# A hybrid encoder layer on one core: for 17 weight units of the down projection, the low half is made by an accumulating DMA

## The chip, the cores and the metric

The kernel runs on one core of one Trainium2 chip. The metric is the device time of one execution in microseconds (us), taken as the median of several runs. The engines are called PE (TensorE), DVE (VectorE), ACT (ScalarE), POOL (GpSimd) and SP (SyncE, which here only issues DMAs). The core has 16 DMA engines, which all its DMA queues share.

## The reference, cut to what matters

One layer over 256 tokens of width 2048: an input projection to eight groups of 1024 columns, two parallel head groups (a gated recurrence and a differential attention), an output projection with residual, then a SwiGLU feed-forward part with 5632 hidden columns:

```
mixed = jnp.concatenate([o_hg, o_da], axis=-1)
x = x + jnp.einsum('bsc,cd->bsd', mixed, w_out[l])
h = rmsnorm(x, norm_ffn_w[l])
u = jax.nn.silu(jnp.einsum('bsd,df->bsf', h, w_gate[l])) * jnp.einsum('bsd,df->bsf', h, w_up[l])
x = x + jnp.einsum('bsf,fd->bsd', u, w_down[l])
```

All of it is in float32. The change touches only the last line, the down projection.

## The kernel before, in words

**Products.** Every projection keeps its accuracy by splitting both operands into a high part, rounded to the format fp32r in which PE multiplies, and a low part, which is the rest. `product` (in the section printed below) makes three matmuls for each pair of a weight row block and a token block: high by high, high activation by low weight, low activation by high weight. These are lines 304, 305 and 306 of the profile. A matmul has 128 x 128 weights of PE (the activations) and 512 moving columns (the model's weights).

**Units.** The model's weights come in units of 128 partitions x 1024 numbers, 4 KB per partition and 512 KB in all. A unit holds two row blocks (KU = 2) of 512 columns (NC). There are 256 tokens in two blocks, so one unit feeds 2 x 2 x 3 = 12 matmuls. `Stream` hands out the units in the order of the whole program: input projection, output projection, gate and up weights in turns, and at the end 88 units of the down weights. These are four chunks (NCH_D) of 512 output columns with 22 units each; they are called chunk 0 to chunk 3 here.

**What a unit goes through.** `load` issues its DMA on SP's queue (L86) into one of five buffers named `raw`. `split` rounds it on ACT into `hi`, profile name whi (L98), and subtracts on DVE `lo` = `raw` - `hi`, profile name wlo (L99). The tiles whi and wlo have three buffers each. After the DVE subtraction the raw buffer is free for the unit five places on. `next`, called when `product` comes to unit u, first calls load up to u + 6 and then split up to u + 1.

**What sets the order.** The code runs in a framework that tracks which instruction needs which data, puts in the waits, and schedules each engine's queue from a list: what is ready first in its own timeline goes first, and the splits stand under a higher priority. So an engine's order need not be the order of the code. Each queue then runs strictly in its order on the chip. Side work (transposes, heads) is spread through the products by `pump`; in the down projection only chunk 0 has any. At the end of each chunk DVE adds the accumulators to the residual `xsb` (L650) and SP stores them (L651).

**Space.** The split activations of the feed-forward part, h2_hi and h2_lo, are two tiles of 128 x 16 x 256 numbers (tags "hhi" and "hlo"). They are last read by the last up product, just before the down projection.

Of the kernel before, what the change touches and what calls it, by code (L numbers as in the profile page):

```python
# [11 lines left out]
F32 = mybir.dt.float32  # L12
F32R = mybir.dt.float32r
BF16 = mybir.dt.bfloat16
U8 = mybir.dt.uint8
AF = mybir.ActivationFunctionType
ALU = mybir.AluOpType
# [3 lines left out]
P = 128  # L21
SEQ = 256
TT = SEQ // P
NC = 512
# [6 lines left out]
X_CUTS = [2, 2]  # L31
KU = 2
RAW_BUFS, HL_BUFS, HAT_BUFS = 5, 3, 5
EVERY_IN, EVERY_OUT, EVERY_FFN, WIDTH = 1, 1, 2, 2
LB_FLOOR = 1e-30
LB_CEIL = 1.0 - 1e-6
# [9 lines left out]
def encoder_layer(ctx: ExitStack, tc: tile.TileContext, xT, xr, w_in, w_out, w_gate, w_up, w_down,  # L46
                  nmix_w, params,
                  dist, masks, out):
    nc = tc.nc
    NK = xT.shape[1]  # L50
# [4 lines left out]
    NCH_D = w_out.shape[0]  # L55
    NF = w_gate.shape[0]
    NKF = NF * HPC
# [5 lines left out]
    big = ctx.enter_context(tc.tile_pool(name="big", bufs=1))  # L63
# [9 lines left out]
    class Stream:  # L73
        def __init__(self, srcs):
            self.srcs, self.raw, self.parts = srcs, {}, {}
            self.nl = self.ns = self.at = 0

        def cuts(self, u):

# [2 lines left out]
        def load(self, upto):  # L82
            while self.nl <= min(upto, len(self.srcs) - 1):
# [3 lines left out]
                self.raw[self.nl] = raw  # L87
                self.nl += 1

        def split(self, upto):  # L90
            self.load(upto)
            while self.ns <= min(upto, len(self.srcs) - 1):
                raw = self.raw.pop(self.ns)
                hi = wpool.tile([P, KU, NC], F32R, tag="whi", name="whi", bufs=HL_BUFS)
                lo = wpool.tile([P, KU, NC], F32R, tag="wlo", name="wlo", bufs=HL_BUFS)
                with tc.high_priority():
                    for k in self.cuts(self.ns):
                        nc.scalar.copy(out=hi[:, k, :], in_=raw[:, k, :])  # L98
                        self.last_split = nc.vector.tensor_tensor(out=lo[:, k, :], in0=raw[:, k, :],  # L99
                                                                  in1=hi[:, k, :].bitcast(F32), op=ALU.subtract)  # L100
                self.parts[self.ns] = (hi, lo)
                self.ns += 1
# [24 lines left out]
    srcs = []  # L127
# [15 lines left out]
    stream = Stream(srcs)  # L143
# [16 lines left out]
    for n in X_CUTS + [KG] * (NKG - 1):  # L160
# [4 lines left out]
        upto = min(-(-k0 // KU) - 1, RAW_BUFS - 1)  # L165
# [124 lines left out]
    def product(a_hi, a_lo, ks, accs, every):  # L290

        nu = len(ks) // KU
        slot = 0
        for i in range(nu):
            whi, wlo = stream.next()
            for tt in range(TT):
                acc = accs[tt]
                for k in range(KU):
                    kk = ks[i * KU + k]
                    hi = a_hi[:, kk, tt * P:(tt + 1) * P]  # L300
                    lo = a_lo[:, kk, tt * P:(tt + 1) * P]
                    first = i == 0 and k == 0
                    last = i == nu - 1 and k == KU - 1
                    nc.tensor.matmul(out=acc, lhsT=hi, rhs=whi[:, k, :], start=first, stop=False)  # L304
                    nc.tensor.matmul(out=acc, lhsT=hi, rhs=wlo[:, k, :], start=False, stop=False)  # L305
                    nc.tensor.matmul(out=acc, lhsT=lo, rhs=whi[:, k, :], start=False, stop=last)  # L306
                    slot += 1
                    if every and slot % every == 0:
                        pump()

    def new_accs(other=False):
        pool, tag = (ps_sc, "sc") if other else (ps_mm, "mm")
        return [pool.tile([P, NC], F32, tag=tag, name="acc") for _ in range(TT)]
# [307 lines left out]
    def put_u(f, u):  # L621

        ut = ffn.tile([P, HPC, SEQ], F32, tag="ut", name="ut")
        yield from squares(ut, u)
        for k2 in range(HPC // 2):
            us = ut[:, k2 * 2:k2 * 2 + 2, :]
            ksl = slice(f * HPC + k2 * 2, f * HPC + k2 * 2 + 2)
            nc.scalar.copy(out=u_hi[:, ksl, :], in_=us)
            nc.vector.tensor_tensor(out=u_lo[:, ksl, :], in0=us, in1=u_hi[:, ksl, :].bitcast(F32), op=ALU.subtract)
            yield  # L630

    for f in range(NF):
        accs = new_accs()
        product(h2_hi, h2_lo, list(range(NK)), accs, EVERY_FFN)
        u = ffn.tile([P, TT, NC], F32, tag="u", name="u")
# [6 lines left out]
                                           in1=u[:, tt, :], op0=ALU.mult, op1=ALU.mult)  # L642
        side.append(put_u(f, u))

    for c in range(NCH_D):
        accs = new_accs(other=c % 2 == 0)
        product(u_hi, u_lo, list(range(NKF)), accs, EVERY_FFN if c == 0 else 0)
        for tt in range(TT):
            xs = xsb[:, tt, c * NC:(c + 1) * NC]
            nc.vector.tensor_tensor(out=xs, in0=accs[tt], in1=xs, op=ALU.add)  # L650
            nc.sync.dma_start(out=out[tt * P:(tt + 1) * P, c * NC:(c + 1) * NC], in_=xs)  # L651
# [53 lines left out]
```

## Time and profile before

| what | value |
|---|---|
| median of 3 runs | 1246.73 us (1246.51 to 1247.34) |
| the profiled execution, its own time | 1247.31 us |
| its span, first to last instruction | 1245.5 us |
| around the span | 1.8 us |
| PE busy | 1233.1 us, 99% of the span |
| DVE, ACT, POOL busy | 862.0, 644.2, 36.6 us |
| granted TensorE clock | 1.000, the upper level (2.4 GHz), in the whole span |

The profile is one execution. Busy is the time in which an engine has an instruction running; for PE the recorded matmuls overlap (each lasts some 390 ns, and a new one begins every 227 ns), so the pace is read from start to start. "Idle before" in a row is the time the engine stood before these instructions, and the name behind the arrow is who ended it. Landing of a DMA is the time from its issue to the arrival of all its data.

### The profile page before, as it was taken

How to read it: one execution, taken by the hardware profiler on the slowest of the kernel's cores; microseconds unless marked ns; L12 is line 12 of the kernel's file. 1: busy time of each engine (PE TensorE's matmuls, PEld its weight loads, DVE VectorE, ACT ScalarE, POOL GpSimd, SP SyncE). 2: the span in 40 equal slices, each digit the busy share in tenths (PEclk: the TensorE clock that was granted, in tenths of full speed). 3: DMA queues.
4: the chain of work that ended last, by engine and by line, in shares of the span. 5: the costliest groups of instructions: out<-in, count | busy, mean ns of one | idle time of the engine just before them, and what ended most of it. 6: DMA issues, size and time to landing. Idle time of an engine off the chain costs nothing.

```text
span 1245.5 us, 15502 instructions
## 1 busy us (share of the span) xinstructions
PE 1233.1 (99%) x5661; PEld 1019.6 (82%) x5661; DVE 862.0 (69%) x1286; ACT 644.2 (52%) x933; POOL 36.6 (3%) x42
## 2 busy tenths in 40 slices
PE   8999999999999999999999999999999999999998
PEld 6778887878888888888888888888888888888887
DVE  6698989698998965757657766765776674444443
ACT  6656755766775665654344344434434443433332
POOL 0000111000012000000000000000000000000000
PEclk9999999999999999999999999999999999999999
DMA  8755345436444555555655556555655556656662
GB/s 300 261 193 169 136 136 186 169 136 202 153 136 152 169 169 169 174 194 190 197 190 192 197 189 200 189 198 189 195 192 192 196 192 197 205 199 206 192 213 86
DMA packets 64812, 230.48 MB, mean 185 GB/s; under 512 B 7264, under 2 KB 7392, under 8 KB 64736
## 3 DMA queue, kind: packets, MB, share of 16 engines
q1 hardware_dynamic: 64592, 229.49, 56.0%
q8 instruction: 44, 0.72, 0.2%
q14 instruction: 32, 0.26, 0.1%
q10 hardware_dynamic: 144, 0.01, 0.0%
HBM read 227.37 MB, written 2.10 MB: 184 GB/s over the span
## 4 chain that ended last, share of the span: by engine, by line
PE 88%; DVE 7%; DMA 1%; issue 1%; ACT 1%; POOL 0%; SPq 0%; ACTq 0%; DVEq 0%; POOLq 0%
PE acc L305 28%; PE acc L306 28%; PE acc L304 28%; DVE wlo L99 3%; DVE zt L327 3%; PE sc L401 2%; ACT whi L98 1%; DMA xt<-in_xT 1%; DMA vec<-in_params 1%; PE oa L510 1%; PE og L435 0%; PE tpx L605 0%; DMA raw<-in_w_in 0%; PE sca L476 0%; PE sca L478 0%
## 5 line engine op out<-in xcount | busy, mean ns | idle before, releaser
L99 DVE TENSOR_TENSOR wlo<-raw,whi 128x1024 fp32r<-128x1024 f32 (+1 forms) x425 | 518.7, 1221 | 342.7 <-ACT whi L98 341.0
L98 ACT CAST whi<-raw 128x1024 fp32r<-128x1024 f32 (+1 forms) x425 | 445.9, 1050 | 508.9 <-PE acc L306 486.5
L305 PE MATMUL acc<-wlo,h_hi 128*128 128x512 f32 x1216 | 476.3, 392 | 4.4 <-DVE wlo L99 4.2
L306 PE MATMUL acc<-whi,h_lo 128*128 128x512 f32 x1216 | 473.6, 391 | 0.0
L304 PE MATMUL acc<-whi,h_hi 128*128 128x512 f32 x1216 | 439.2, 393 | 1.5 <-ACT whi L98 1.5
L305 PEld LDWEIGHTS acc<-wlo,h_hi 128*128 128x128 f32 x1216 | 228.4, 188 | 55.7 <-DVE wlo L99 10.3
L304 PEld LDWEIGHTS acc<-whi,h_hi 128*128 128x128 f32 x1216 | 227.9, 188 | 48.1 <-ACT whi L98 2.7
L306 PEld LDWEIGHTS acc<-whi,h_lo 128*128 128x128 f32 x1216 | 228.4, 188 | 46.5
L305 PE MATMUL acc<-wlo,u_hi 128*128 128x512 f32 x352 | 136.9, 389 | 0.0
L306 PE MATMUL acc<-whi,u_lo 128*128 128x512 f32 x352 | 136.9, 389 | 0.0
L304 PE MATMUL acc<-whi,u_hi 128*128 128x512 f32 x352 | 122.9, 389 | 0.0
L327 DVE STREAM_TRANSPOSE ut<-u 32x256 f32<-32x256 f32 x176 | 76.7, 436 | 3.4
L305 PEld LDWEIGHTS acc<-wlo,u_hi 128*128 128x128 f32 x352 | 66.1, 188 | 13.8
L306 PEld LDWEIGHTS acc<-whi,u_lo 128*128 128x128 f32 x352 | 66.1, 188 | 13.7
L304 PEld LDWEIGHTS acc<-whi,u_hi 128*128 128x128 f32 x352 | 66.0, 188 | 13.7
L327 DVE STREAM_TRANSPOSE zt<-z 32x256 f32<-32x256 f32 x160 | 69.7, 436 | 2.8
L305 PE MATMUL acc<-wlo,m_hi 128*128 128x512 f32 x128 | 50.4, 394 | 0.0
L306 PE MATMUL acc<-whi,m_lo 128*128 128x512 f32 x128 | 50.0, 392 | 0.0
L304 PE MATMUL acc<-whi,m_hi 128*128 128x512 f32 x128 | 48.8, 396 | 0.0
L388 DVE TENSOR_TENSOR pk<-pk,t 128x256 f32<-128x256 f32 x112 | 44.0, 451 | 2.0 <-ACT hat L380 1.8
L380 ACT COPY hat<-pk 128x512 f32<-128x512 f32 x56 | 35.7, 666 | 11.8 <-PE sc L401 5.6
L401 PEld LDWEIGHTS sc<-hat 128*128 128x128 f32 x224 | 30.2, 191 | 2.6
(129 smaller groups left out, 641.0 us busy)
## 6 DMA issues: line engine op xcount, KB each, us to landing
raw<-in_w_in SPq DMA_DIRECT2D x127, 512.0 KB, 3.7
raw<-in_w_gate SPq DMA_DIRECT2D x88, 512.0 KB, 4.3
raw<-in_w_up SPq DMA_DIRECT2D x88, 512.0 KB, 4.4
raw<-in_w_down SPq DMA_DIRECT2D x88, 512.0 KB, 4.4
raw<-in_w_out SPq DMA_DIRECT2D x32, 512.0 KB, 3.7
xsb<-in_xr SPq DMA_DIRECT2D x4, 512.0 KB, 6.3
out<-xsb SPq DMA_DIRECT2D x8, 256.0 KB, 5.7
xt<-in_xT SPq DMA_DIRECT2D x3, 512.0 KB, 8.2
```

The lines of the kernel that those rows point to most:

```text
L98: nc.scalar.copy(out=hi[:, k, :], in_=raw[:, k, :])
L99: self.last_split = nc.vector.tensor_tensor(out=lo[:, k, :], in0=raw[:, k, :], in1=hi[:, k, :].bitcast(F32), op=ALU.subtract)
L304: nc.tensor.matmul(out=acc, lhsT=hi, rhs=whi[:, k, :], start=first, stop=False)
L305: nc.tensor.matmul(out=acc, lhsT=hi, rhs=wlo[:, k, :], start=False, stop=False)
L306: nc.tensor.matmul(out=acc, lhsT=lo, rhs=whi[:, k, :], start=False, stop=last)
L327: nc.vector.transpose(out=d, in_=s)
L380: nc.scalar.copy(out=sub_ap(hat, 0, [[SEQ, 2], [2 * m, nb], [m, 2], [1, m]]), in_=sub_ap(pk, 0, [[2 * SEQ, 2], [2 * m, nb], [SEQ + m, 2], ...
L388: nc.vector.tensor_tensor(out=ap, in0=ap, in1=tap, op=ALU.mult)
L401: nc.tensor.matmul(out=sc[:, j, :], lhsT=kk[:, js], rhs=qq[:, js], start=True, stop=True)
L510: nc.tensor.matmul(out=o[:, tt, :], lhsT=st[:, j, tt * P:(tt + 1) * P], rhs=v[:, j, cs], start=j == 0, stop=j == TT - 1)
```

## The change

Seventeen units of the down projection (in chunk 1 every fourth of the 22 units, six in all; in chunk 2 every second, eleven in all) are split in another way. ACT rounds raw into hi as before, then ACT writes the negative of hi into lo, and an accumulating DMA issued from POOL adds raw onto lo inside SBUF. Their hi and lo stand in four pairs of slots of their own, in the place of h2_hi and h2_lo. This is done up to three units (AHEAD) before the split of the ordinary units. Chunks 0 and 3 stay as they are.

```
+AHEAD = 3
...
+            self.slots, self.by_dma = [], set()
...
+        def split_by_dma(self, u):
+
+            raw = self.raw.pop(u)
+            hi, lo = self.slots[self.nd % len(self.slots)]
+            self.nd += 1
+            with tc.high_priority():
+                nc.scalar.copy(out=hi, in_=raw)
+                nc.scalar.activation(out=lo, in_=hi.bitcast(F32), func=AF.Copy, scale=-1.0)
+                nc.gpsimd.dma_start(out=lo, in_=raw, accum_op=ALU.add)
+            self.parts[u] = (hi, lo)
+
         def split(self, upto):
             self.load(upto)
+            for u in sorted(self.by_dma):
+                if u <= upto + AHEAD and u < self.nl and u in self.raw and self.slots:
+                    self.split_by_dma(u)
             while self.ns <= min(upto, len(self.srcs) - 1):
+                if self.ns in self.parts:
+                    self.ns += 1
+                    continue
                 raw = self.raw.pop(self.ns)
...
+    d_hi = big.tile([P, NK * SEQ // (KU * NC), KU, NC], F32R, tag="hhi", name="d_hi")
+    d_lo = big.tile([P, NK * SEQ // (KU * NC), KU, NC], F32R, tag="hlo", name="d_lo")
+    stream.slots = [(d_hi[:, i], d_lo[:, i]) for i in range(NK * SEQ // (KU * NC))]
+    per = NKF // KU
+    first = len(srcs) - NCH_D * per
+    stream.by_dma = {first + per + i for i in range(0, per, 4)} | {first + 2 * per + i for i in range(0, per, 2)}
     for c in range(NCH_D):
```

## Rows read from the trace of the kernel before

**Rows 1.** The page, busy time, share of the span and instructions of each engine.
```profile
PE   1233.1 (99%) x5661; PEld 1019.6 (82%) x5661; DVE 862.0 (69%) x1286; ACT 644.2 (52%) x933; POOL 36.6 (3%) x42
```

**Rows 2.** Busy time by stretch, chunks 1, 2, 3; columns in the first line.
```profile
core 0: us, PE busy (x) PEld busy (x) DVE busy (x) ACT busy (x) POOL busy (x), PEclk, DMA share, GB/s
1061.80:1121.60 59.80, 59.80 (x265) 49.51 (x264) 28.11 (x25) 23.17 (x23) 0.00 (x0) 1.00 0.63 203
1121.60:1181.40 59.80, 59.80 (x265) 49.55 (x264) 28.12 (x25) 23.18 (x22) 0.00 (x0) 1.00 0.63 202
1181.40:1241.20 59.80, 59.80 (x264) 49.18 (x263) 26.00 (x23) 21.10 (x20) 0.00 (x0) 1.00 0.48 150
```

**Rows 3.** Timeline in chunk 1: PE, start and length of a unit's first pair.
```profile
1102.33 0.61 PE L304 MATMUL acc<-whi,u_hi 128*128 128x512 f32 x2
...
1105.05 0.61 PE L304 MATMUL acc<-whi,u_hi 128*128 128x512 f32 x2
...
1113.21 0.61 PE L304 MATMUL acc<-whi,u_hi 128*128 128x512 f32 x2
```

**Rows 4.** Groups of instructions by line, chunk 2 (1121.6 to 1181.4 us).
```profile
L99 DVE TENSOR_TENSOR wlo<-raw,whi 128x1024 fp32r<-128x1024 f32 x22 | 27.0, 1225 | 31.7 <-ACT whi L98 31.7
L98 ACT CAST whi<-raw 128x1024 fp32r<-128x1024 f32 x22 | 23.2, 1055 | 36.6 <-PE acc L306 36.6
```

**Rows 5.** Timeline of all engines in chunk 1: splits and loads.
```profile
1111.78 1.22 DVE L99 TENSOR_TENSOR wlo<-raw,whi 128x1024 fp32r<-128x1024 f32 x1 [1.49 <-ACT whi L98]
...
1113.03 3.05 SPq L86 DMA_DIRECT2D raw<-in_w_down  x2
...
1113.41 1.05 ACT L98 CAST whi<-raw 128x1024 fp32r<-128x1024 f32 x1 [1.67 <-PE acc L306]
...
1114.50 1.23 DVE L99 TENSOR_TENSOR wlo<-raw,whi 128x1024 fp32r<-128x1024 f32 x1 [1.50 <-ACT whi L98]
```

**Rows 6.** DMA queues and issues, chunk 2 (window 1121 to 1181 us).
```profile
q1 hardware_dynamic: 3483, 12.13, 62.8%
...
raw<-in_w_down SPq DMA_DIRECT2D x22, 512.0 KB, 4.5
out<-xsb SPq DMA_DIRECT2D x2, 256.0 KB, 5.4
```

**Rows 7.** Line 86 from 1040 to 1220 us: landing of its 66 loads.
```profile
DMA to landing us min/median/max: 3.1/4.4/6.4
```

**Rows 8.** DMA, the first 100 us in 40 slices of 2.5 us.
```profile
DMA  2999999997568999999860546165438288666656
GB/s 45 272 299 360 398 418 415 387 403 265 174 190 288 280 387 376 249 287 370 364 208 11 200 177 213 46 210 174 152 123 301 88 297 320 185 205 229 206 151 224
...
xt<-in_xT SPq DMA_DIRECT2D x3, 512.0 KB, 8.2
```

**Rows 9.** Timeline of all engines up to the start of chunk 0.
```profile
999.17 1.05 ACT L98 CAST whi<-raw 128x1024 fp32r<-128x1024 f32 x1 [1.67 <-PE acc L306]
...
1000.26 1.23 DVE L99 TENSOR_TENSOR wlo<-raw,whi 128x1024 fp32r<-128x1024 f32 x1 [1.49 <-ACT whi L98]
...
1001.40 0.74 DVE L641 SCALAR_TENSOR_TENSOR u<-acc,rstd,u 128x512 f32<-128x512 f32 x1
...
1001.69 0.39 PE L304 MATMUL acc<-whi,u_hi 128*128 128x512 f32 x1
```

**Rows 10.** Timeline of ACT in chunk 0: a slice of u_hi is written.
```profile
1021.89 1.14 ACT L628 CAST u_hi<-ut 128x512 fp32r<-128x512 f32 x2
```

More of the change, by code (lines that the diff above doesn't have):

```diff
@@ L75, in __init__ @@
             self.srcs, self.raw, self.parts = srcs, {}, {}
-            self.nl = self.ns = self.at = 0
+            self.nl = self.ns = self.at = self.nd = 0
+            self.slots, self.by_dma = [], set()
         def cuts(self, u):
```

## The prediction

> **What bounds the kernel now.** I first read the page's busy times [rows 1]: PE is busy for 99% of the span, DVE for 69%, ACT for 52%. A share over the whole span says little about the last stage, so I then cut the down projection into its chunks [rows 2]. In chunks 1 and 2, which the change touches, PE is busy for 59.80 of 59.80 us, at the full granted clock; DVE is busy for 28.1 us, ACT for 23.2, POOL for nothing, and the DMA engines for 63%. The timeline gives the pace [rows 3]: units begin at 1102.33, 1105.05 and, three later, 1113.21, so one unit takes 2.72 us, 22 units make 59.84 us, and that is the chunk's whole length. PE waits for nothing here. What the change takes off DVE is therefore off a path that ends early, and the question is only what it puts on.
>
> How early the path ends [rows 5]: two units before a unit is needed, a whi buffer comes free and ACT rounds (1113.41, 0.2 us after the unit of 1113.21 began); DVE ends at 1115.73. SP issues the load of the unit five places on right behind that, as the 1113.03 behind the 1113.00 shows. So ordinary low parts are there 2.9 us before PE wants them (2 x 2.72 - 2.5), and the load of unit w is issued 0.2 us before the start of w - 6 and lands, with 4.5 us [rows 6], 1.6 us after the start of w - 5. It is rounded only 0.2 us after the start of w - 2, so raw data lie ready for 6.8 us.
>
> **The change, part by part.** *Removed:* 17 subtractions of 1.225 us on DVE [rows 4], 20.8 us. DVE stood idle for 31.7 us of chunk 2 waiting for ACT, and PE never waited for it. Worth nothing to the end.
>
> *Added on ACT:* 17 more passes over 128 x 1024. The row for such a pass is the rounding, 1.055 us [rows 4], so 17.9 us, against 36.6 us in which ACT waited for PE in chunk 2 alone. Hidden in sum. In time: a DMA unit holds ACT for 2.1 us; an ordinary rounding that becomes ready at 0.2 us behind it would end 2.1 us later than now, inside the 2.9 us. Nothing, as long as ACT does not stand waiting for a load with an ordinary rounding queued behind it (a rival, below). The slots are slices of one tile; that the framework tracks slices is seen in chunk 0, where a slice of u_hi is written without a wait while PE reads others [rows 10]. So a slot waits for PE only where its own last unit, eight units back in chunk 2, is unread; that is long past.
>
> *Added on POOL's queue:* 17 DMA issues. POOL has nothing else to do there [rows 2], so nobody stands behind them. No row shows how long it takes to issue one: it goes into the latency below.
>
> *Added on the DMA engines:* 17 transfers of 512 KB that read raw, read lo and write lo. The trace has no accumulating transfer. Bounds come from the loads. One pass over 512 KB costs, by the share in chunk 2 (62.8% of 60 us for 12.13 MB [rows 6]), 37.7 x 0.524 / 12.13 = 1.63 us of all 16 engines; in the fullest stretch, five slices from 10 to 22.5 us at a mean of 404 GB/s [rows 8], 524288 / 404000 = 1.30 us. Low end: one pass, if the second read runs beside the first, 1.3 us. I take two passes, because the add must fetch two operands that are each as large as a load: 2.6 to 3.3 us. High end: four passes, 6.5 us, if the add itself goes slower than the bytes; nothing in the rows excludes it.
>
> A rule of the Trainium skill speaks to this price and against the change: "Collectives: The Full Stack", section "The bandwidth ceiling: the fold count and why AG ≠ RS ≠ AR", says that a reduction in the DMA engine needs two source reads, both on the same ring, and so delivers half the rate of a copy. By it the price would be the two passes, and no run here shows it yet.
>
> Now the budget. In chunk 1 four units (10.88 us) carry four loads and one add: 5 x 1.63 + 1.63 = 9.8 us. It fits. In chunk 2 two units (5.44 us) carry two loads and one add: 4 x 1.63 = 6.5 us, which is 1.08 us too much, eleven times, 11.9 us; or at the full stretch's rate 4 x 1.30 = 5.2 us, which just fits at 96%.
>
> The latency: a DMA unit's raw lands 1.6 us after the start of w - 5, two ACT passes and hand-overs take 2.2, so the add is issued at 3.8, and 5 x 2.72 - 3.8 = 9.8 us are left until PE starts w. A second limit holds in chunk 2, since raw stays taken until the add has landed. The load of w + 5 waits for that, the load of w + 6, again a DMA unit's, stands behind it on SP's queue, then come landing (4.5), ACT (2.2) and its own add. For six units in 16.3 us the add may take 16.3 - 0.35 - 4.5 - 2.2 = 9.2 us. What will it take? At least 3.1 us, as the fastest load [rows 7]. Loads take 4.5, and a second pass makes it 6.1: no wait. Where the queues were full, loads took 8.2 [rows 8]; with a second pass of 1.3 that is 9.5, just too long.
>
> **The sum.** Chunk 2 with two passes is the part that pays. At the full stretch's rate it fits, and only the latency limit is missed by 0.3 us per six units, some 1 us in all. At the share of the stage it lacks 11.9 us, of which the first 3.7 (9.8 - 6.1, the lead of a DMA unit) are used up unseen: 8.2 us. The loads of this stage are paced, so their share is likely to shrink somewhat when the queue is full, but the add is a new kind of traffic: I take 5 us, between the ends. Chunk 3 only catches up. The profiled execution, 1245.5 us of span and 1.8 around it, would become 1247.3 + 5.0 = 1252.3; it stands 0.6 above the median of the three runs, so the forecast is 1251.7 us.
>
> **The rivals.** *The add is hidden (no change).* If both reads and the write overlap, an add costs near one pass, chunk 2 needs 3 x 1.63 = 4.9 of 5.44 us, the add lands in about 5 us, and PE goes on at 2.72 us per unit: 1246.7. For it speaks that PE has no idle at all and each stage of the pipe has over 3 us of lead. The point from which it decides is the 5.44 us per pair and the 9.2 us of landing. The Trainium skill, "DMA: Bandwidth & Descriptors", section "Anatomy of one DMA — SWDGE (gpsimd) path", gives a POOL-issued transfer 2.0 us plus its bytes at 436 GB/s; by it a plain 512 KB copy would take 3.2 us, an estimate, and the latency would be no limit; no row has such a transfer.
>
> *The add is much slower than two passes.* At three, a pair takes 2 x 1.63 + 4.9 = 8.2 us, 2.7 over, eleven times 30; chunk 1 lacks 0.5 five times; less 3.7 of lead it is some 29 us: 1276. At four, 4.3 x 11 + 2.2 x 5 - 3.7 = 55: 1302. For it: no row has an add in a transfer. Against it: nothing but that the data volume asks for two.
>
> *ACT waits for loads.* In the code the DMA unit's rounding (up to u + 4) stands ahead of the ordinary one (u + 1). Were ACT's queue kept in that order, ordinary rounding, subtraction, load five on, and the two ACT passes would form a ring per pair in chunk 2: 1.06 + 1.23 + 4.5 + 2.1 = 8.9 us against 5.44, eleven times 3.45, less 3.7: +34, 1281. Against it: the scheduler takes what is ready. Where chunk 0 begins (1001.69), the subtraction for a unit two ahead ran at 1000.26, before L641 at 1001.40, though the code has L641 first [rows 9]; and an ordinary rounding is ready 0.2 us after a unit's start, a DMA unit's load lands 1.6 after one.
>
> *Faster.* PE has no idle in the stage, so only something outside it could give time; I see nothing. *That the change is not carried out* I exclude: at next(u) loads are known up to u + 6 and the ordinary splits stand at u + 1, so each of the 17 units is in raw when the test for u + 4 comes.
>
> **How the numbers follow.** A measurement of this kernel tells some 0.2%, 2.5 us, from no change. Forecast case (two passes, +1 to +8): 0.38, of which 0.05 lies within 2.5 us. Hidden: 0.34. Slow add: 0.16, half of it at three passes or less. ACT order: 0.09. Faster: 0.03. So slower 0.58, same 0.39, faster 0.03. The forecast case alone spans 1247.7 to 1255. The range starts at 1246.0, takes in the hidden case, and reaches to three passes, 1276; left out are the four-pass half (0.08), ACT order (0.09) and faster (0.03), 0.2 together.
>
> **What would show it.** Right: in chunk 2 the DMA share is at 0.9 or more, adds land in 8 to 11 us, PE shows idle time released by the adds there and none in chunk 1 or 3, and loads land later than 4.5 us. The hidden case: chunk 2 still lasts 59.8 us. Slow add: chunk 1 is longer too. ACT order: ACT's idle in chunk 2 is ended by raw loads, with adds landing early. The forecast is wrong if chunk 2 keeps its length, or if the wait is on anything but the adds.

## The result, and the profile after the change

The changed kernel took 1266.49 us (median of 4 runs, 1265.57 to 1267.48) beside 1246.81 for the kernel before (4 runs, 1246.51 to 1247.34): a ratio of 1.0158, with an interval of 1.0140 to 1.0175. That is 19.7 us slower, where the prediction had 5. The profiled execution took 1267.48 us with a span of 1265.7, 20.2 more than before in both.

First the page of the changed kernel: busy times, the group of the new roundings and the row of the adds among its DMA issues (KB each, median us to landing).

```profile
PE 1241.1 (98%) x5661; PEld 1022.2 (81%) x5661; DVE 840.8 (66%) x1269; ACT 658.0 (52%) x950; POOL 51.6 (4%) x59
...
L98 ACT CAST d_hi<-raw 128x1024 fp32r<-128x1024 f32 x17 | 17.8, 1049 | 76.8 <-DMA raw<-in_w_down 76.8
...
d_lo<-raw POOLq DMA_DIRECT2D x17, 512.0 KB, 7.1
```

Against [rows 1], DVE lost the predicted 21 us of work, and ACT was given 14. The line to stop at is the second: before 15 of the 17 new roundings ACT stood still until a load of raw weights had landed, for 76.8 us in all. In chunk 2 of the kernel before, roundings had waited for PE alone [rows 4].

Next chunks 0 to 3, by the windows view of the changed kernel, each from its first matmul to that of the next (a chunk has 264; the x counts also one that reaches into the stretch). Two short stretches inside chunk 2 follow.

```profile
core 0: us, PE busy (x) PEld busy (x) DVE busy (x) ACT busy (x) POOL busy (x), PEclk, DMA share, GB/s
1001.75:1061.87 60.12, 60.12 (x266) 49.47 (x264) 34.94 (x41) 24.98 (x25) 1.06 (x1) 1.00 0.62 189
1061.87:1134.50 72.63, 64.15 (x265) 50.16 (x264) 20.35 (x18) 29.37 (x30) 6.11 (x7) 0.98 0.73 210
1134.50:1201.66 67.16, 62.78 (x265) 51.38 (x264) 16.59 (x15) 30.29 (x30) 7.84 (x9) 0.95 0.97 273
1201.66:1261.50 59.84, 59.84 (x265) 49.36 (x263) 25.89 (x22) 21.10 (x20) 0.00 (x0) 1.00 0.44 146
...
1150.00:1165.00 15.00, 14.85 (x54) 12.02 (x55) 2.75 (x3) 6.13 (x7) 2.11 (x3) 0.81 0.98 276
...
1180.00:1190.00 10.00, 10.00 (x46) 8.28 (x45) 2.30 (x2) 6.04 (x7) 1.74 (x2) 1.00 1.03 297
```

Chunks 0 and 3 keep their length, but for 0.3 us. Chunk 1 takes 72.6 us and chunk 2 takes 67.2, where each took 59.8 [rows 2]: 12.8 and 7.3 us more, so the 20 us are all there, and most of them in chunk 1. Two things in these rows speak against the forecast. Chunk 1, which was to fit, has a PE idle for 8.5 us (72.63 - 64.15) while the DMA engines are busy for only 0.73 of the time. And from 1180 to 1190 us, at a DMA share of 1.03, PE has no idle at all.

PE's idle in the two chunks is 8.5 + 4.4 = 12.9 us. Of the other 7, some 4.3 go to matmuls at the lower clock. The rest are late starts that are not counted as idle, since a matmul is recorded as busy for some 390 ns and the next can begin after 227. The timeline of PE in the changed kernel (start, length, and in brackets the idle before and its releaser) shows the longest case:

```profile
1145.38 0.39 PE L323 MATMUL acc<-d_hi,u_hi 128*128 128x512 f32 x1
1150.15 0.79 PE L324 MATMUL acc<-d_lo,u_hi 128*128 128x512 f32 x1 [4.38 <-DMA d_lo<-raw]
1150.74 0.63 PE L325 MATMUL acc<-d_hi,u_lo 128*128 128x512 f32 x1
1151.17 0.63 PE L323 MATMUL acc<-d_hi,u_hi 128*128 128x512 f32 x1
```

Matmuls that began every 0.227 us begin every 0.43 behind the 4.38 us of idle, and the 15 us around them have a granted clock of 0.81: part of the stretch ran at 1.2 rather than 2.4 GHz. Thirteen matmuls ran so here and eight in chunk 1 (from 1118.2 to 1121.6 us the granted clock was 0.51). At 0.2 us more for each of the 21, that makes the 4.3 us.

Who is waited for? The waits of the changed kernel from 1055 to 1266 us (us in total, times, longest):

```profile
ACT d_hi L98 <- DMA raw<-in_w_down: 74.1, 14, 9.3
...
PEld acc L324 <- DMA d_lo<-raw: 8.2, 4, 4.8
...
PE acc L324 <- DMA d_lo<-raw: 6.5, 3, 4.4
PEld acc L323 <- ACT whi L117: 5.1, 3, 2.3
PEld acc L324 <- DVE wlo L118: 4.0, 5, 1.1
```

PE waits for adds three or four times, but as often for ordinary units, which no add touches: for ACT's whi and for DVE's wlo. Those are late because ACT was. The timeline of ACT in chunk 1 of the changed kernel shows how:

```profile
1076.28 1.05 ACT L98 CAST d_hi<-raw 128x1024 fp32r<-128x1024 f32 x1 [7.71 <-DMA raw<-in_w_down]
1077.23 1.04 ACT L117 CAST whi<-raw 128x1024 fp32r<-128x1024 f32 x1
1078.18 1.06 ACT L99 ACTIVATE d_lo<-d_hi 128x1024 fp32r<-128x1024 f32 x1
1079.14 1.98 ACT L117 CAST whi<-raw 128x1024 fp32r<-128x1024 f32 x2
1087.53 1.05 ACT L98 CAST d_hi<-raw 128x1024 fp32r<-128x1024 f32 x1 [6.41 <-DMA raw<-in_w_down]
1088.61 1.06 ACT L99 ACTIVATE d_lo<-d_hi 128x1024 fp32r<-128x1024 f32 x1
1089.58 1.98 ACT L117 CAST whi<-raw 128x1024 fp32r<-128x1024 f32 x2
1099.57 1.05 ACT L98 CAST d_hi<-raw 128x1024 fp32r<-128x1024 f32 x1 [8.02 <-DMA raw<-in_w_down]
...
1113.69 1.04 ACT L98 CAST d_hi<-raw 128x1024 fp32r<-128x1024 f32 x1 [9.28 <-DMA raw<-in_w_down]
```

This is the picture to remember. ACT stands for 6 to 9 us in front of a DMA unit's rounding whose data have not landed. The moment it gets through, the ordinary roundings queued behind run one after the other with no idle between: they had been ready, and stood behind an instruction that was not. Four units pass from one L98 to the next, and four units are 10.88 us of PE's work; from 1076.28 to 1113.69 the mean is 12.5.

The chain of waits of the changed kernel, in order of time (start, length, what), tells why the loads come late:

```profile
1088.61 1.07 ACT d_lo L99
...
1089.97 4.83 DMA d_lo<-raw
...
1094.81 4.74 DMA raw<-in_w_down
...
1099.57 0.04 ACT d_hi L98
...
1101.47 1.06 ACT d_lo L99
...
1102.82 7.08 DMA d_lo<-raw
...
1109.91 3.75 DMA raw<-in_w_down
...
1113.69 0.04 ACT d_hi L98
```

Negative, add, next load, next rounding: the load at 1094.81 starts when the add of 1089.97 lands, since it gets the raw buffer that this add was reading. The waits of SP's queue between 1045 and 1201 us say the same of all 17:

```profile
SPq L88 <- DMA d_lo<-raw: 67.4, 17, 8.2
```

Chunk 2 loses its time in one place, the 4.38 us of idle above. The chain there, by the same view:

```profile
1124.53 8.67 DMA d_lo<-raw
...
1133.22 5.85 DMA raw<-in_w_down
...
1142.35 7.76 DMA d_lo<-raw
...
1150.15 0.79 PE acc L324
```

The add of unit 44 (unit 0 is the first of the down projection) lands at 1133.20. Only then can the load of unit 48 start, which gets its buffer, and the add of unit 48 lands too late for PE. Unit 48 lasts from 1145.38 to 1155.01, 9.6 us in the place of 2.72: that is 6.9 of the 7.3 us of chunk 2.

From this came the theories for the experiments. **Theory A**: a ring through ACT's queue. A DMA unit's rounding waits there for its load, the ordinary roundings wait behind it, and the next DMA unit's load needs a buffer that those free. **Theory R**: what costs is the raw buffer that the add holds until it has landed. **Theory B**, that of the prediction: the DMA engines have more to move than fits.

### The profile page after: what moved, and what is told of

The parts are those of the page before. It is cut to its first block, busy times and chain, and to the rows that moved or that the text cites. A ratio compares the mean times of both kernels' runs of the same rounds, so it can differ in the third digit from the quotient of the medians.

```text
span 1265.7 us, 15537 instructions
## 1 busy us (share of the span) xinstructions
PE 1241.1 (98%) x5661; PEld 1022.2 (81%) x5661; DVE 840.8 (66%) x1269; ACT 658.0 (52%) x950; POOL 51.6 (4%) x59
## 4 chain that ended last, share of the span: by engine, by line
PE 79%; DMA 8%; DVE 8%; issue 2%; ACT 2%; SPq 0%; POOL 0%; ACTq 0%; POOLq 0%; DVEq 0%
PE acc L324 25%; PE acc L325 25%; PE acc L323 25%; DVE wlo L118 4%; DMA raw<-in_w_down 3%; DVE zt L346 3%; DMA d_lo<-raw 3%; PE sc L420 2%; ACT whi L117 1%; DMA xt<-in_xT 1%; DMA vec<-in_params 1%; PE oa L529 1%; DMA xsb<-in_xr 0%; ACT d_lo L99 0%; PE og L454 0%
## 5 line engine op out<-in xcount | busy, mean ns | idle before, releaser
L118 DVE TENSOR_TENSOR wlo<-raw,whi 128x1024 fp32r<-128x1024 f32 (+1 forms) x408 | 497.5, 1221 | 381.4 <-ACT whi L117 379.8
L117 ACT CAST whi<-raw 128x1024 fp32r<-128x1024 f32 (+1 forms) x408 | 427.3, 1049 | 438.0 <-PE acc L325 415.2
L324 PE MATMUL acc<-wlo,u_hi 128*128 128x512 f32 x284 | 111.9, 394 | 2.5 <-DVE wlo L118 2.5
L325 PE MATMUL acc<-whi,u_lo 128*128 128x512 f32 x284 | 111.1, 391 | 0.0
L323 PE MATMUL acc<-whi,u_hi 128*128 128x512 f32 x284 | 105.4, 394 | 3.8 <-ACT whi L117 3.8
L323 PEld LDWEIGHTS acc<-whi,u_hi 128*128 128x128 f32 x284 | 53.7, 189 | 16.4 <-ACT whi L117 5.1
L324 PEld LDWEIGHTS acc<-wlo,u_hi 128*128 128x128 f32 x284 | 53.9, 190 | 15.1 <-DVE wlo L118 4.0
L325 PEld LDWEIGHTS acc<-whi,u_lo 128*128 128x128 f32 x284 | 53.9, 190 | 11.3
L98 ACT CAST d_hi<-raw 128x1024 fp32r<-128x1024 f32 x17 | 17.8, 1049 | 76.8 <-DMA raw<-in_w_down 76.8
```

The source lines that it names most:

```text
L98: nc.scalar.copy(out=hi, in_=raw)
```

## The experiments

All ratios are to the kernel before, run beside each; the interval is 95%. Where an edit touches the down projection's splits, the scheduler writes ACT's queue anew, so what each kernel's queue is has to be read, not assumed. In the built programs it runs like this around units 30 and 34 of the down projection (D a DMA unit's rounding, neg its negative, N an ordinary rounding):

```
as changed                N27 D30 N28 neg N29 N31 D34 neg N32 N33
order                     N27 D30 neg N28 N29 N31 D34 neg N32 N33
add by DVE                N25 D30 neg N27 N28 N29 D34 neg N31 N32
narrow add                N25 D30 N27 neg N28 N29 D34 neg N31 N32
own raw, in order         N25 D30 neg N27 N28 N29 D34 neg N31 N32
later rounding            N27 N28 D30 neg N29 N31 N32 D34 neg N33
own raw, later rounding   N27 N28 D30 neg N29 N31 N32 D34 neg N33
own raw, 33 adds          N27 D30 neg N29 D32 neg N31 D34 neg N33
```

**The order in ACT's queue.** The DMA unit's rounding is issued behind the ordinary roundings that stand in the code at the same place.

```
             with tc.high_priority():
-                nc.scalar.copy(out=hi, in_=raw)
+                with tc.issue_after(self.last_cast.ins):
+                    nc.scalar.copy(out=hi, in_=raw)
...
-            for u in sorted(self.by_dma):
-                ...
             while self.ns <= min(upto, len(self.srcs) - 1):
...
+                        self.last_cast = nc.scalar.copy(out=hi[:, k, :], in_=raw[:, k, :])
...
+            for u in sorted(self.by_dma):
+                ...
```

> The ordinary rounding of the same step is put ahead of the DMA unit's on ACT's queue; the loads that wait for an add then are those of the next DMA unit itself (four in a row in chunk 1). Theory R (a ring through the raw buffer that an add holds: add 7.1 us, load 4.5, two ACT passes 2.2, POOL's hand-over 0.3, 14.1 us per four units against 10.88): chunk 1 stays long or gets longer, total 1264 to 1275 us. Theory A (ACT's queue: ordinary roundings stuck behind a rounding that waits for its load): chunk 1 falls back towards 60 us, total under 1258. Theory B (DMA bandwidth alone): as the changed kernel, 1266.

Measured: 1258.39 us, 1.0094 (1.0079 to 1.0109), which is 11.2 slower than before instead of 19.7. That is 0.4 us over what theory A allowed, and less than R and B had. With the same DMAs and the same work, the order is worth 8.5 us, so B, to which the order makes no difference, can't be the whole. But less moved in chunk 1 than was meant. At units 22, 38 and 42 the rounding did come behind an ordinary one. At 26 and 30 only the negative moved: it follows its rounding directly, so the add is issued one ordinary rounding (1.04 us) sooner. At 34 nothing moved. An add that is issued sooner also ends its hold sooner, so this run does not part A from R. Chunk 1 still takes 67.05 us here and chunk 2 66.62, and ACT still waits 66.2 us for loads.

**The add made by DVE.** The same work on ACT, but no transfer.

```
-                nc.gpsimd.dma_start(out=lo, in_=raw, accum_op=ALU.add)
+                nc.vector.tensor_tensor(out=lo, in0=raw, in1=lo.bitcast(F32), op=ALU.add)
```

> Same ACT work and order, but the add is done by DVE (about 1.2 us) in place of the DMA; the raw buffer is free again after it, and the DMA engines carry the loads alone. Theory R and theory B: 1247 to 1250 us, chunks 1 and 2 at 60 us each. Theory A: still long, 1258 to 1270, with ACT idle until raw loads land while ordinary roundings stand behind.

Measured: 1253.0 us, 1.0049 (1.0033 to 1.0066): 5.8 slower than before with not one accumulating DMA. All three had missed: R and B had it too low, A too high. The loss is all in chunk 1, which takes 67.28 us; chunk 2 takes 59.84. The queue is not quite that of the changed kernel: the rounding stands one place earlier (D30 ahead of N27). The chain of waits of this kernel in chunk 1 shows the ring bare:

```profile
1078.78 6.51 DMA raw<-in_w_down
...
1085.32 1.06 ACT d_hi L98
...
1086.39 1.07 ACT d_lo L99
...
1089.77 1.23 DVE wlo L118
...
1091.01 6.66 DMA raw<-in_w_down
...
1097.69 1.06 ACT d_hi L98
```

From one d_hi to the next, 12.37 us: two passes on ACT (2.1), the way through DVE's queue to the end of an ordinary subtraction (3.5, with its waits), and a load of 6.66. In the kernel before, a load took 4.4 [rows 7]. It is longer here, probably because the three ordinary units, let go together, free their buffers together: SP issued four loads within 3.7 us from 1088.74. With 4.4 in the place of 6.66 the ring would be 10.1 us and fit into 10.88. No run took the bunching away by itself.

**Own raw buffers for the DMA units.** The add then holds nothing that another load needs.

```
+                if self.nl in self.by_dma:
+                    raw = self.dpool.tile([P, KU, NC], F32, tag=("u", "ut")[self.nr % 2], name="raw")
+                    self.nr += 1
...
+    stream.dpool = ffn
```

> The DMA units load into four raw buffers of their own (in tiles of the feed-forward part that are free by then), so an add holds no buffer of the ring of five, and their loads come far ahead, so that ACT does not wait for them. Adds and bytes as in the changed kernel. Theories R and A: chunk 1 back at 60 us. Theory B for chunk 2 (6.2 to 6.5 us of DMA work per pair against 5.44): chunk 2 still 5 to 10 us long, total 1252 to 1257; without B 1247 to 1249.

Measured: 1255.18 us, 1.0065 (1.0050 to 1.0080). The loss moved. Chunks 1 and 2 both take 59.84 us, the full pace, with all 17 adds, where B had chunk 2 long. Chunk 0 takes 67.60: its PE is busy for only 54.57 of the 59.80 us to 1061.5, at a DMA share of 0.89. The loads into the free buffers were all issued early, in a bunch. The roundings of chunk 1's DMA units came early in ACT's queue with them, and ACT stood in front of four of these for 16.3 us. So the order changed along with the buffers, and the experiment was made again below with the loads in order.

**A narrow add.** Only the first 64 of 512 columns of each row block are added, 64 KB instead of 512.

```
+                nc.gpsimd.dma_start(out=lo[:, :, :64], in_=raw[:, :, :64], accum_op=ALU.add)
```

> The DMA adds only the first 64 of the 512 columns of each row block (the rest of the low part is left at minus the high part), an eighth of the bytes; ACT's work and order and the raw buffers as in the changed kernel. Theory B: 1247. Theory R: the add lands in some 4 us instead of 7.1, the ring of chunk 1 shrinks from 12 to under 10 us, total 1247 to 1254. Theory A: near 1260 or more.

Measured: 1261.3 us, 1.0117 (1.0100 to 1.0134). With an eighth of the bytes, 14.1 of 19.7 us remain, so B falls as the whole. These adds still took 4.8 us to land (median, 7.1 for the full ones). By chunks, chunk 2 is whole again (59.84 us) and chunk 1 is not better at all (72.54 beside 72.63). The queue is not that of the changed kernel either: in chunk 1 the roundings of units 30 and 34 stand one place earlier, so what the shorter hold gave there can't be told.

**A later rounding.** AHEAD is 2, with the order of the first experiment: a DMA unit's rounding comes behind that of the ordinary unit two places before it (N28 ahead of D30).

```
-AHEAD = 3
+AHEAD = 2
```

> AHEAD 2, and the DMA unit's rounding is tied behind the ordinary rounding of the unit two before it on ACT's queue; raw buffers, adds and bytes as in the changed kernel. Theory A (the loss is a ring: rounding of a DMA unit waits for its load, ordinary roundings queue behind it, and the load of the next DMA unit waits for a buffer that those free): one ordinary rounding fewer in the ring and the load less early needed, so the ring falls below 10.88 us per four units; total 1247 to 1253 us. Theory R (raw buffers held by the adds) and theory B (bandwidth): still 1258 or more, chunk 2 over 64 us.

Measured: 1252.22 us beside 1246.53, 1.0051 (1.0036 to 1.0066). ACT's waits for loads fall to 42.0 us. What is left stands before the adds: PE's two queues wait for them for 8.6 and 6.1 us. The total is as A had it, but by chunks only half of it: chunk 1 is nearly whole at 61.15 us, and chunk 2 still takes 66.28, as R and B had said (over 64). In chunk 2, where every second unit is a DMA unit, the edit moves little in the queue, and nothing from D52 on.

**Own raw buffers, loads in order.** As the third experiment, and each of these loads is issued behind the one before it.

```
+                    with tc.issue_after(self.last_load.ins) if self.nl in self.by_dma else ExitStack():
+                        self.last_load = nc.sync.dma_start(out=raw[:, k, :], in_=self.srcs[self.nl][:, k, :])
```

> As the run with raw buffers of their own, but the DMA units' loads keep their place in the order of loads instead of coming early in a bunch. The ring of five then serves ordinary units alone. Theories A and R: no ring is left, chunks 1 and 2 at 60 us each, total 1247 to 1249 us, with all 17 adds done. Theory B: chunk 2 longer, 1252 or more.

Measured: 1254.0 us, 1.0060 (1.0045 to 1.0075), a miss by 5 us of the time expected for it. Taking the hold away leaves 7.5 of the 19.7 us. Chunk 2, with the same adds and bytes, is whole at 59.84 us; the loss is in chunk 1, at 67.21. There ACT's roundings for DMA units start at 1069.04, 1080.88, 1092.47 and 1104.37, still 11.6 to 11.9 us apart, each behind 6.2 to 6.9 us of waiting for the load. So the ring of the DVE experiment is there without any hold. The queue is the likely reason of the miss (the tenth experiment bears it out): free of the hold, the DMA unit's rounding was put one place earlier than in the changed kernel, with three ordinary roundings behind it.

**Own raw buffers, 33 adds.** The same with every second unit of chunks 1, 2 and 3, so that only one ordinary rounding stands behind each DMA unit's, and nearly twice as many adds run.

```
+    stream.by_dma = {first + j * per + i for j in (1, 2, 3) for i in range(0, per, 2)}
```

> The same with every second unit of chunks 1, 2 and 3 as DMA units, 33 adds. It asks whether two loads and one add per 5.44 us fit the DMA engines over 180 us. Two passes at the stage's 1.63 us (6.5 us per pair): 33 x 1.08 - 10 = 25 us over before, 1272. At the full stretch's 1.30 (5.2 us per pair): it fits, 1247 to 1250.

Measured: 1246.93 us (10 runs) beside 1246.53 (13 runs), 1.0002 (0.9992 to 1.0012): nothing lost. Its first and its last 20 us of seven such stretches by the windows view (columns as above):

```profile
1061.50:1081.50 20.00, 20.00 (x90) 16.54 (x89) 6.01 (x6) 10.10 (x10) 2.61 (x3) 1.00 1.04 307
...
1181.40:1201.40 20.00, 20.00 (x90) 16.57 (x89) 5.59 (x5) 11.24 (x11) 3.48 (x4) 1.00 1.05 311
```

The DMA share is at 1.04 to 1.05 for 140 us on end, adds land in 8.5 us (median, up to 12.2), loads in 10.9, and PE has no idle. Two loads and an add per pair of units fit.

**A copy in the place of the add.** As the sixth experiment, with the low part overwritten by raw itself, to price the add.

```
-                nc.gpsimd.dma_start(out=lo, in_=raw, accum_op=ALU.add)
+                nc.gpsimd.dma_start(out=lo, in_=raw)
```

> As e6, but the POOL DMA copies raw over the low part instead of adding (the low part is then raw itself; the add alone is left out). The share of the DMA engines per transfer: if an add costs two passes and a copy one, 2.8 us per add against 1.4 to 1.6 per copy, and the landing shorter by 1 to 2 us. Time as e6.

Measured: 1251.23 us, one run. Its POOL queue from 1055 to 1200 us (packets, MB, share of 16 engines; then the issues, with the median landing):

```profile
q0 software_dynamic: 2304, 8.39, 15.7%
...
d_lo<-raw POOLq DMA_DIRECT2D x16, 512.0 KB, 5.5
```

and the same rows of the sixth experiment:

```profile
q0 software_dynamic: 2304, 8.39, 29.8%
...
d_lo<-raw POOLq DMA_DIRECT2D x16, 512.0 KB, 8.5
```

For the same 16 transfers a copy costs 0.157 x 145 / 16 = 1.42 us of the 16 engines, an add 0.298 x 145 / 16 = 2.70: a factor of 1.9.

**The two passes on POOL.** Nothing of the DMA units is left in ACT's queue.

```
+                nc.gpsimd.tensor_copy(out=hi, in_=raw)
+                nc.gpsimd.tensor_scalar(out=lo, in0=hi.bitcast(F32), scalar1=-1.0, scalar2=None, op0=ALU.mult)
```

> The DMA unit's two passes (rounding, negative) run on POOL in place of ACT, so ACT's queue holds ordinary roundings alone and nothing stands behind a DMA unit that waits for its load; five shared raw buffers and all 17 adds as in the changed kernel. Theory A (ACT's queue closes the ring): total 1247 to 1252 us, PE without idle in chunk 1. Theory R (the raw buffers held by adds are enough): 1257 or more.

Measured: 1272.55 us, 1.0203 (1.0183 to 1.0222). By the total, theory A missed by over 20 us and R's bound is met, but POOL is slow at this work. The groups of POOL (busy, mean ns) from 1050 to 1210 us:

```profile
L99 POOL TENSOR_SCALAR d_lo<-d_hi 128x1024 fp32r<-128x1024 f32 x17 | 52.4, 3110 | 0.6
L98 POOL CAST d_hi<-raw 128x1024 fp32r<-128x1024 f32 x16 | 19.0, 1185 | 53.4 <-DMA raw<-in_w_down 51.4 <-PE acc L325 2.0
```

A negative takes 3.1 us where ACT took 1.06, and in chunk 2, which takes 84.92 us, the adds come too late. But chunk 1 is nearly cured, though its adds hold shared buffers too: it takes 61.17 us (72.63 after the change). Taking the passes out of ACT's queue did that, together with the other order in which the shared buffers are then handed out.

**Own raw buffers and the later rounding together.**

> Raw buffers of their own with loads in order (as e6) and the DMA unit's rounding one ordinary rounding later on ACT's queue (as e5). Theory A: both halves of the ring of chunk 1 are shortened, 1246 to 1249 us. If instead a late add is what costs: the adds are issued up to 2.7 us later, PE would wait for d_lo in chunk 1 and the total stays at 1251 or more.

Its edit is that of the fifth and the sixth. Measured: 1247.87 us (10 runs) beside 1247.27 (14 runs), 1.0006 (0.9996 to 1.0015): all 17 adds are there and no loss that can be told. The timeline of ACT in its chunk 1:

```profile
1070.48 1.05 ACT L120 CAST whi<-raw 128x1024 fp32r<-128x1024 f32 x1 [1.67 <-PE acc L331]
1071.43 1.05 ACT L104 CAST d_hi<-raw 128x1024 fp32r<-128x1024 f32 x1
...
1081.36 1.05 ACT L120 CAST whi<-raw 128x1024 fp32r<-128x1024 f32 x1 [1.67 <-PE acc L331]
1082.31 1.05 ACT L104 CAST d_hi<-raw 128x1024 fp32r<-128x1024 f32 x1
```

Set it beside the ACT rows of the changed kernel. The d_hi rounding now starts without idle, right behind an ordinary one, every 10.88 us; the idle is released by PE again, as in [rows 4].

**Chunk 1 alone, chunk 2 alone.** by_dma keeps one of its two sets.

```
+    stream.by_dma = {first + per + i for i in range(0, per, 4)}
```

> Only the six units of chunk 1 (every fourth) go by DMA. Theory A: the ring of 12 us per four units against 10.88 costs most of what the changed kernel loses in chunk 1, some 6 to 10 us: 1253 to 1257 us.

```
+    stream.by_dma = {first + 2 * per + i for i in range(0, per, 2)}
```

> Only the eleven units of chunk 2 (every second) go by DMA, from a pipe that has its full lead. If the two chunks' losses add up, 1247 + 19.7 less what chunk 1 alone costs, so 1256 to 1260 us; if chunk 2 lost mainly because chunk 1 had used up the lead, 1247 to 1252 us.

Measured: 1255.98 us, 1.0076 (1.0057 to 1.0096), for chunk 1 alone; 1254.67 us, 1.0057 (1.0039 to 1.0075), for chunk 2 alone. The first is as expected, the second lies between its two cases. That is 8.7 and 7.4 over the 1247.27 beside them, 16.1 together, against 19.7. The six units of chunk 1 cost about as much as the eleven of chunk 2, the contrary of what a budget of bytes would give. The other 3.6 do not look like a lead that chunk 2 lacked: chunk 1 takes 67.78 us with its own six units alone and 72.63 in the changed kernel, where the first units of chunk 2 already stand in ACT's queue before chunk 1 ends (D44 ahead of N41). That this is the reason was not shown.

**What stands.** Four kernels make a table of the two causes, in us over the kernel before of the same job:

| | order left to the scheduler | DMA unit's rounding tied behind the ordinary one two units before |
|---|---|---|
| raw buffers shared | 19.7 | 5.7 |
| own raw buffers, loads in order | 7.5 | 0.6 |

The left column is not one order (its lower kernel has the rounding a place earlier), the right one is, in chunk 1. Either cure alone removes more than half, and only both remove it.

The two chunks tell why it takes both. These are their lengths in us in the profiled executions, one of each kernel (up to 3.2 us from the kernel's median time):

| | chunk 1 | chunk 2 |
|---|---|---|
| before | 59.84 | 59.84 |
| as changed | 72.63 | 67.16 |
| order | 67.05 | 66.62 |
| later rounding | 61.15 | 66.28 |
| the two passes on POOL | 61.17 | 84.92 |
| narrow add | 72.54 | 59.84 |
| add by DVE | 67.28 | 59.84 |
| own raw, in order | 67.21 | 59.84 |
| own raw, later rounding | 60.31 | 59.84 |

Chunk 2 is whole wherever no add holds a shared buffer, or holds it shorter, and nowhere else. There the cause is theory R, the raw buffer that is held until the add has landed. Chunk 1 comes near its length only where ACT's queue is another. There theory A is a cause: a ring of latencies of load, rounding and negative in ACT's queue, the ordinary roundings held up behind, and the next load. The two kernels with own buffers show it, since up to the end of chunk 1 their loads and buffers are the same and only ACT's order differs: 67.21 against 60.31.

How much the hold adds in chunk 1 of the changed kernel is open. The framework hands the shared buffers out anew in each kernel. In the changed one the loads of units 26, 38 and 42 get the buffer of the DMA unit before them (the chain of 1088.61 to 1113.69 above goes through such holds), and in the kernel of the later rounding no load of chunk 1's DMA units does, so that its 61.15 us are not the order's work alone.

No version beat the kernel before. The best two equal it, as they must with a PE that had no idle.

## Why the prediction was right and wrong

*What was taken away is worth nothing.* Right. DVE's 21 us are gone and no chunk is shorter for it.

*ACT's 17 passes are hidden.* In sum, yes: ACT stays at 52% of the span, and with all 17 passes the tenth experiment loses nothing. In place, no. This step carried the failure in chunk 1, which lost 12.8 of the 20 us: "Nothing, as long as ACT does not stand waiting for a load with an ordinary rounding queued behind it". That is what it did there. The rival for it had a chance of 0.09, because "the scheduler takes what is ready" and a DMA unit's load was reckoned to land later than an ordinary rounding becomes ready. The scheduler does so in its own timeline, and the queue that it wrote has the DMA unit's rounding first. Why its timeline has it so is open. What was shown is that tying it behind the ordinary rounding of the unit two before it, with own buffers, cures the loss.

The rival was also priced wrongly. Its ring went once per pair of chunk 2 (8.9 us for 5.44) and had no part in chunk 1. In truth one ring spans four units in chunk 1 and lasts 11.6 to 12.4 us even without the held buffer, with loads of 6.5 to 6.7 us in it (the chain of the DVE experiment), issued four together. The rival's time of 1281 was too high, and its place, chunk 2 alone, was wrong.

*The second limit of chunk 2*, that raw stays taken until the add has landed, was seen and rated at 1 us. This is the other step that failed: it is what chunk 2 lost, 7.3 us, and chunk 2 is whole in every kernel without it. The prediction had the load of the unit five on wait for the add, and so counted six units, 16.3 us, for one round. In the changed kernel the load of unit 48 waited for the add of unit 44. The round had four units, 10.88 us, and took 17.8 (from one add's issue to the other's, 1124.53 to 1142.35). At the later rounding the hold is worth 5.1 us in all (5.7 against 0.6).

*Two passes per add.* Right: 2.70 us in the sixth experiment and, from 33.1% of 145 us for 17 transfers, 2.82 in the changed kernel, inside the 2.6 to 3.3. A copy took 1.42. The Trainium skill ("Collectives: The Full Stack", section "The bandwidth ceiling: the fold count and why AG ≠ RS ≠ AR") states for the reduction of a collective that its add needs two source reads and so delivers half the rate of a copy; the factor of 1.9, of a plain accumulating DMA, agrees with it.

*The budget of chunk 2 lacks 1.08 us per pair.* This is the term from which the 5 us came, and it was wrong in whole. Under a full queue a load of the seventh experiment costs 0.548 x 145 us for 30.40 MB, 1.37 us per 512 KB, near the low end of 1.30 and not the 1.63 of a paced queue; its add costs 2.65. Two loads and an add are 5.39 of 5.44 us. "At the full stretch's rate it fits" was the right end, and the middle between the two was no safe choice: the share of a paced queue was no price here.

*The add's latency.* 7.1 us median, 4.8 to 9.1, below the first limit of 9.8 and the forecast of 8 to 11. The estimate from "DMA: Bandwidth & Descriptors" of the Trainium skill, section "Anatomy of one DMA — SWDGE (gpsimd) path", 3.2 us for a copy, is below the 5.5 that the copies of the eighth experiment took beside the loads.

*What would show it.* The list did its work: the DMA share of chunk 2 is above 0.9, as forecast, but chunk 1 has idle, PE waits for more than the adds, and "ACT's idle in chunk 2 is ended by raw loads" was the sign of the rival that came true. A DMA share near 1 was a poor test by itself, for the seventh experiment has it with no loss.

The total lies inside the range, and on the side given the highest chance, by luck. The range went up to 1276 for the sake of a slow add, and the add was not slow; the 20 us came from a rival held at 0.09, in a chunk where it was not expected, and from a limit rated at 1 us that chunk 2 alone was to have. By its own last sentence ("or if the wait is on anything but the adds") the forecast was wrong.

## What to carry to other kernels

Work that is free in sum on an idle engine still has a place in that engine's queue: when it waits there for a transfer, ask who is queued behind it, and whether those free the buffer that the next such transfer needs. If so, write down the ring (landing, passes, the queue behind) and compare it with PE's time for the same units, using the landing of loads that are issued in a bunch. A buffer that an accumulating DMA reads is held until it has landed, 7 us here: make a ring of that too, or give it a buffer of its own. Look at the loss chunk by chunk, cut where the work changes: one total hid two causes here; and price a transfer by the fullest stretch of the trace, not by the share of a paced one.

## What was not expected of the hardware

- An accumulating DMA of 64 KB took 4.8 us to land (median), one of 512 KB 7.1: two thirds of the time for an eighth of the bytes.
- The DMA engines held a share of 1.04 to 1.05 for 140 us, loads landing in 10.9 instead of 4.4 us, without any cost to PE.
- POOL needs 3.1 us for the negative of 128 x 1024 numbers and 1.2 us to round as many; ACT needs 1.06 and 1.05.
- Behind 4.4 us of idle, 13 matmuls of PE ran at the lower clock (1150.15 to 1155.8 us). With eight others in chunk 1 that cost 4.3 of the 20 us.
